# Moving h and the second layer's head outputs within SBUF in a float32 two-layer backbone

## The chip, the cores and the metric

The kernel runs on one core of a Trainium2 chip. The metric is the device time of one execution in microseconds (us), the median of several runs. The engines are named as the profile names them: PE is TensorE's products and PEld its weight loads, DVE is VectorE, ACT is ScalarE, POOL is GpSimd, SP is SyncE, whose queue issues most of the DMA transfers. SBUF is the on-chip memory of 128 partitions that products read their operands from, PSUM the memory that they write to.

## The reference, cut to what matters

Two layers over 512 latent tokens `x` and 256 context tokens `ctx`, 1024 channels each. The first layer mixes by gated linear attention, the second by an mLSTM; each ends in a convolutional feed-forward block (ConvFFN). All of it is float32.

```
for i in range(2):
    h_c = rmsnorm(ctx, ...) * (1 + sc1_c) + sh1_c          # modulated norms
    h_l = rmsnorm(x, ...)   * (1 + sc1_l) + sh1_l
    o_c, o_l = gla_mixer(h_c, h_l, ...) if i == 0 else mlstm_mixer(h_c, h_l, ...)
    x = x + g1_l * o_l                                     # a mixer ends in (heads * gate) @ w_out
    h_l = rmsnorm(x, ...) * (1 + sc2_l) + sh2_l
    x = x + g2_l * conv_ffn(h_l, ...)                      # (gelu(conv(h @ w_g)) * (h @ w_a)) @ w_down
    ...                                                    # layer 0: the same for ctx
return rmsnorm(x, final_norm_g)
```

The mixers' inputs (queries, keys, values, gates of 4 heads) are products of h with columns of one large matrix. `w_g` and `w_a` are 1024 x 2816, `w_down` is 2816 x 1024.

## The kernel before

**Products.** Activations lie channel-major: the partition is the channel within a block of 128, the free axis is the token, 256 context tokens first and then 512 latent ones. A float32 product is made of three passes over operands split in two (hi and lo): `mm3` (lines 308 to 310) issues hi by hi, hi by lo, lo by hi. In `nc.tensor.matmul(ps, l, r)` the first operand is the stationary one, 128 columns that a weight load (PEld) brings into PE, and the second the moving one, of 256 or 512 columns here. While PE streams one product it loads the next one's weights.

**h** is the modulated norm, held as two tiles `hhi_` and `hlo_` of [128, 8, 768] float32 (`new_h`). For `projT_steps` the moving operand is row k of h over the latent tokens (512 columns, 1,024 bytes into the row) or over the context (256 columns, at the row's begin), and the weights are stationary. For the values (`v_proj`, and `values` at the start) it is the other way: 128 tokens of h are stationary, the weights move.

**Where tiles lie.** Pools are handed out from the bottom of SBUF, each tile at a multiple of 32 bytes. The constants' pool (`self.pc`) starts at byte 16,512 of a partition with `ident` (512 bytes), `ones` (128), `eps` and `junk` (32 each); then come `xl` (16,384), `xc` (8,192), `hhi_` and `hlo_` (24,576 each), and behind them the small tables, `A01` and `mgb` among the last. Then comes the pool of the large weights, with slots of 4,096 bytes. A row of h has 3,072 bytes and a block of 128 weight columns 512, so within 512 bytes all rows of a tile, both token ranges and all weight blocks begin at the same place. The places that matter, by the program's own allocation:

| tile | used by | first byte | place within 512 |
|---|---|---|---|
| `hhi_`, `hlo_` (h) | `fg`, `fa`, `fs`, `fsc`, `gr`, `gk`, `gq`, `mk`, `mq`, `mo` move it; the values keep it stationary | 41,792 and 66,368 | 320 |
| rings `whi`, `wlo` (large weights) | stationary for the products just named but half of `fs`, `fsc`; stationary for the output projections of heads 0 to 2 | 107,936 on | 416 |
| `ahi`, `alo` and `wh_d`, `wl_d` (layer 0) | moving and stationary of `fd`; half of `fs`, `fsc` has its weights in `wh_d`'s ring | 189,632 and 150,720 on | 192, both |
| the same, layer 1 | the same | 188,576 and 149,664 on | 160, both |
| `hhi`, `hlo` of the heads, layer 0 | moving in the output projection `po` | 215,968 on | 416 |
| `hhi`, `hlo` of the heads, layer 1 | the same | 212,224 on | 256 |
| `xl`, `xc` (the residual) | no product's operand | 17,216 and 33,600 | 320 |

Head 3's output projection has its weights in slots of other tiles (96 in the first layer; 320, 0 and 96 in the second).

**Names of products.** In the ConvFFN `fg` is h by the gate weights and `fa` h by the value weights, for each of 22 blocks of 128 channels; `fs` and `fsc` are the same for the first two blocks (latent halves and context); `fd` is the down product. In the first layer's scans `gk`, `gq`, `gr` are keys, queries and the output gate of a head, in the second's `mk`, `mq`, `mo`; `vpsgv` and `vpsmv` are the values, `v01p` those of heads 0 and 1 at the start. `po` is the output projection; its number gives layer, head and block, its letter the tokens (`L` all 512 latent ones, `C` the context).

**Order.** PE's order is the program's. In the mixers the steps of a head's scan are interleaved by hand with other products (`Filler`): values, output gate, queries and keys of the next head, and the last head's output projection. In the ConvFFN, `up` issues the gate products of a block, the convolution on VectorE (9 steps of 512 columns, line 1418), the value products, and every few blocks `down`, whose results VectorE adds to the residual (`update`, line 553). Three PSUM banks serve the down products, so a late update holds PE up.

Of the kernel before, what the change touches and what calls it, by code (L numbers as in the profile page):

```python
"""Two-layer hybrid backbone (gated linear attention, then mLSTM, each with a ConvFFN).

Activations are kept channel-major: partition = channel within a block of 128, free = token.
Float32 products run as three float32r passes: x = hi + lo is an exact split, and
hi*hi + hi*lo + lo*hi carries float32's accuracy.
"""
# [18 lines left out]
P = 128  # L25
D = 1024
KT = D // P
# [16 lines left out]
# the table set with both Exp and Ln  # L44
EXP_LN = "natural_log_exp_and_others"
# share of products between two steps of a scan, by head
# [9 lines left out]
class TwoPools:  # L56
    """One pool to its users; tiles whose tag is listed come from the first pool."""
# [8 lines left out]
class Filler:  # L66
    """Products (generators that yield a rough weight) to run between the steps of a scan.

    A step of side, which waits for its own loads, comes in after each share of `every`."""
# [21 lines left out]
    def through(self, gen):  # L91
        """Run up to the end of gen."""
        while gen in self.gens:
            self.step()
        self.owed = min(self.owed, 0.0)
# [13 lines left out]
class Norm:  # L109
    """rms norm of one 256-token segment in steps that the products of other segments run between."""  # L110
# [7 lines left out]
    def square(self, k):  # L118
        """Squares summed over blocks 0..6, and those of block 7."""
        nc = self.b.nc  # L120
        acc = self.acc[k == KT - 1]
        if k in (0, KT - 1):
            nc.scalar.activation(acc, self.xs[k], AF.Square)
            return
        sq = self.tail.sq[k % 2]
        nc.scalar.activation(sq, self.xs[k], AF.Square)
        (nc.vector if k > 4 else nc.gpsimd).tensor_tensor(acc, acc, sq, op=ALU.add)

    def stat(self, spread=True):
        """1/rms of the tokens: columns of r and, on every partition, PSUM rb [128, 256]."""  # L130
# [15 lines left out]
    def mod(self, k):  # L146
        """Block k of h: normalised x, modulated and split."""
# [22 lines left out]
    def gain(self, k):  # L170
        """Block k times the final gain, turned token-major."""
# [8 lines left out]
    def store(self):  # L180
        """Output rows of the segment: the turned blocks over the rms of their token."""
# [12 lines left out]
class Tail:  # L194
    """The last residual update of a phase, by segments, and the norms that follow it."""
# [14 lines left out]
    def after(self, si, m):  # L210
        """Called when block m of segment si has been updated."""
# [16 lines left out]
        else:  # L228
            # what the segment before left, then its successor's
# [6 lines left out]
class Body:  # L236
# [14 lines left out]
    def start_tile(self, name):  # L251
        """Any of the six banks that the start has for its tiles."""
        self.turn = (self.turn + 1) % 6
        return self.mm_tile(name) if self.turn < 4 else self.aux_tile(name)
# [12 lines left out]
    def split(self, hi, lo, src, bias=None, eng=None):  # L267
        """hi + lo = src (+ bias), exactly; hi, lo are float32r."""
# [8 lines left out]
    def load_w(self, src, name, kind="", bufs=3, later=False, more=None, eng=None):  # L277
        """Weight block src [nk*128, C], and columns more of the same rows, as split [128, nk, C] tiles;
        eng takes the differences."""
# [12 lines left out]
    def w_tile(self, pool, dt, tag, name, bufs, nk, C):  # L292
        """[128, nk, C] in a slot of 1024 columns."""
# [11 lines left out]
    def mm3(self, ps, wl, wr, start, stop):  # L305
        """ps += lhs^T rhs for split operands (hi, lo)."""
# [5 lines left out]
    def projT_steps(self, ps, w, h, cols):  # L312
        """ps [128, n] = (h @ w)^T over the KT blocks; w [128, KT, 128], h [128, KT, TOK]."""
# [9 lines left out]
    def vec_table(self, rows, name, pool=None):  # L323
        """rows: list of DRAM APs [n, 128]; returns a [128, sum n] tile of columns."""
        return self.vec_turn(*self.vec_load(rows, name, pool=pool))
# [62 lines left out]
    def run_late(self, n=9):  # L388
        """Steps of the last norm that were left to the phase that follows."""
# [5 lines left out]
    def ada_setup(self):  # L395
# [7 lines left out]
        self.A = {}  # L403

    def ada_load(self, l, blks, k0, nk, pool):
        """Rows k0.. (nk blocks) of the modulation columns blks."""
# [25 lines left out]
    def ada_piece(self, l, blks, pool, sts):  # L432
        """Modulation blocks blks (4 blocks of 128 channels) of layer l for both streams.

        Column group j of the tensor engine takes block j, so four products run at once."""
# [10 lines left out]
        # block j of the list sits in columns 32 j + stream  # L446
# [7 lines left out]
    def ada_seq(self, parts):  # L454
        """Modulation parts (layer, part) in halves of 512 columns, one row block of weights per step, loaded
        two steps ahead: the rows times their entries of c are summed over the row blocks for each stream, then
        over the partitions on the tensor engine.

        Parts: 0 sh1, 1 sc1, 2 g1, 3 sh2, 4 sc2, 5 g2."""
# [11 lines left out]
        for i, (l, part, half, k) in enumerate(steps):  # L471
# [3 lines left out]
            # the context needs no more after the second layer's mixing  # L475
# [12 lines left out]
            # column group j: blocks 2 q and 2 q + 1 of stream s for j = 2 q + s, or block j of the one stream  # L488
# [27 lines left out]
    def make_A(self, l, which, b0, n, ns=2):  # L516
        """A = g * (1 + sc) for n channel blocks from b0, the first ns streams."""
# [17 lines left out]
    def inv_sqrt(self, r, ss, n):  # L535
        """r = (ss / n + eps) ** -0.5"""
# [4 lines left out]
    def sqrt_next(self, t):  # L541
        """Have the root's table loaded once t, the last result of another function, is there."""
        self.nc.scalar.activation(self.junk, t[:, -1:], AF.Sqrt, bias=self.eps, scale=0.0)

    def x_seg(self, seg):
        """Residual blocks of a 256-token segment: 0, 1 the latent halves, 2 the context."""
# [4 lines left out]
    def update(self, xv, ps, gate):  # L551
        """x += gate * ps"""
        self.nc.vector.scalar_tensor_tensor(xv, ps, gate, xv, op0=ALU.mult, op1=ALU.add)  # L553

    def start(self, pool):
        """The first layer's h, two channel blocks at a time as their modulation comes in; the values of
        heads 0 and 1 are summed up over the blocks on the way. The second half of the latent tokens comes
        in last. Returns the PSUM tiles of the values and the last steps of their sums, one for each pair
        of chunks."""
        nc = self.nc  # L560
        # x over the rms, channel-major: columns ctx, then latent
# [16 lines left out]
        def squares(seg):  # L578
            ss[seg] = pool.tile([P, 2], F32, tag="xss", name=f"xss{seg}", bufs=3)
            for t in range(2):  # L580
                # the squares themselves go where xr comes, in blocks that are still free
# [18 lines left out]
        def spread(*segs):  # L600
            """1/rms on every partition."""
# [12 lines left out]
        def modulate(i, *parts):  # L614
            """Blocks 2 i and 2 i + 1 of h for parts (stream, columns) that lie side by side."""
# [63 lines left out]
    def out_weights(self, l, h, to=None):  # L679
        """Per block of 128 rows: (hi, lo), each two [128, 512] views; to: eight views to take them."""  # L680
# [16 lines left out]
    def out_proj(self, l, h, acts, segs, tail=None, w=None):  # L697
        """x += g1 * (act @ w_out) over the rows of head h; acts[h]: (hi, lo) lists of two blocks."""
# [25 lines left out]
    def head_square(self, pool, l, h, o, p):  # L724
        """Sum of squares of pair p of token-major o."""
        if p == 0:
            self.ss = pool.tile([P, NPAIR], F32, tag="hss", name=f"hss{l}{h}", bufs=2)
        sq = pool.tile([P, DV], BF16, tag="hsq", name=f"hsq{l}{h}{p}", bufs=1)
        self.nc.scalar.activation(sq, o[:, p, :], AF.Square, accum_out=self.ss[:, p:p + 1])

    def head_norm(self, pool, l, h, o, npair):
        """Token-major o [128, npair, DV] of a head over its rms, in place."""
# [6 lines left out]
    def head_gate(self, pool, l, h, o, npair, gate, g, bufs, acts, segs=None):  # L739
        """o transposed, times g and the gate; split into acts[h]. segs: (pair, pairs) to finish one by one."""  # L740
# [29 lines left out]
    def v_proj(self, vt, w_in, col0, name, gates=None):  # L770
        """Token-major values of one head: vt [128, NPAIR, >=DV]. With gates (first column, number, out): those
        columns' products as well, handed to out(p, ps) for each pair of chunks p."""
# [21 lines left out]
    def gla_masks(self, pc):  # L794
        """Keep token j for output i: forward j <= i, backward j >= i; scores are [j, i]."""
# [9 lines left out]
    def scan_mask(self, pool):  # L805
        """1 everywhere, 0 where a chunk starts: for the forward and the backward scan."""
# [6 lines left out]
    def gla_za(self, keep, pool):  # L813
        """Low-rank gate inputs, split and stacked for one product: rows hi, lo, hi."""
        nc, a = self.nc, self.a
        # in the rings of the large weights
# [21 lines left out]
        # gate weights: rows hi, hi, lo; the other direction's rows are zero  # L838
# [10 lines left out]
    def gla_gates(self, pool, h, zs, w2, smask):  # L849
        """exp(+-c), c the log decay of each direction summed from the middle of each pair of chunks,  # L850
        and the factors that carry the state from one pair to the next."""
# [19 lines left out]
        # sums of whole chunks; the half that comes first in its direction counts from its end  # L871
# [4 lines left out]
        # order of pairs 1, 0, 5, 4, 3, 2; g[p] leads out of pair p  # L876
# [18 lines left out]
    def gla_qk(self, pool, h, gates, hats):  # L895
        """Queries and keys of a head, scaled by the decay of each direction, over the gates."""
# [31 lines left out]
    def gla_scan(self, pool, h, hats, vt, steps, scb, free):  # L928
        """Both directions of one head; yields where other products may run. free() makes o's slot free."""
# [67 lines left out]
    def gla(self, vps, last):  # L997
        with ExitStack() as es:
# [10 lines left out]
            with self.tc.tile_pool(name="gla_b", bufs=1) as hpb:  # L1009
# [14 lines left out]
                for h in range(NH):  # L1024
# [14 lines left out]
                    if h == NH - 1:  # L1039
                        # into slots that the last heads have left, to keep the ring of weights for the next phase  # L1040
# [516 lines left out]
```

## Time and profile before

| | |
|---|---|
| median of 3 runs | 1664.98 us (1663.76 to 1666.72) |
| profiled execution: span from the first to the last instruction | 1662.1 us |
| mean granted TensorE clock | 0.992 |
| PE busy | 1625.9 us (98%) |
| VectorE busy | 1256.2 us (76%) |
| ScalarE busy | 673.3 us (41%) |
| first layer's ConvFFN, main part | 440 to 950 us |
| second layer's ConvFFN, main part | 1296 to 1631 us |

The profile gives one execution. Its span leaves out what lies before the first and behind the last instruction; the runs' median is 2.9 us above it. Products are pipelined and the profile models their ends, so the time that a product costs in a stream is the distance from its start to the next one's start, not its listed duration.

### The profile page before, as it was taken

Reading aid. Unit: us, or ns where it says so; the run is one execution under the profiler, and the core shown is the slowest. Engines: PE = TensorE matmul, PEld = TensorE weight load, DVE = VectorE, ACT = ScalarE, POOL = GpSimd, SP = SyncE. Lnnn points to the kernel's source line nnn. Section 1 sums busy time; section 2 is a strip of 40 time slices with the busy share of each in tenths; the row PEclk is TensorE's granted clock in tenths of the full one; section 3 lists DMA queues with packets and bytes.
Section 4 is the critical chain, followed back from the end, with each engine's and each line's share of the span. In section 5 each row is a group of like instructions: output and inputs, shape, how many; then the busy total and the mean of one; then the engine's idle time right before and its main releaser. Section 6 shows DMA issues by size and latency. Waiting matters only on the chain.

```text
span 1662.1 us, 24173 instructions
## 1 busy us (share of the span) xinstructions
PE 1625.9 (98%) x9504; PEld 1398.3 (84%) x9504; DVE 1256.2 (76%) x2139; ACT 673.3 (41%) x1155; POOL 109.2 (7%) x174
## 2 busy tenths in 40 slices
PE   7999999998999999999999999999998999999998
PEld 6778898888988888888888998889878877888887
DVE  5867877868975978686666589776778898777874
ACT  5675444446431314132221366635465333222334
POOL 0011001004000000000000130000002110000001
PEclk9999999999999999999999999999999999999999
DMA  9522443522330523251222125243321233223321
GB/s 311 173 59 72 146 135 109 159 70 60 93 108 26 152 77 115 65 170 53 75 64 65 39 78 151 83 134 102 90 63 51 77 114 102 75 77 102 114 77 51
DMA packets 178614, 163.64 MB, mean 98 GB/s; under 512 B 8860, under 2 KB 146724, under 8 KB 178500
## 3 DMA queue, kind: packets, MB, share of 16 engines
q1 hardware_dynamic: 178132, 161.97, 32.1%
q8 instruction: 74, 1.21, 0.3%
q14 instruction: 40, 0.33, 0.1%
q10 hardware_dynamic: 240, 0.13, 0.0%
q0 software_dynamic: 128, 0.00, 0.0%
HBM read 159.98 MB, written 2.10 MB: 98 GB/s over the span
## 4 chain that ended last, share of the span: by engine, by line
PE 84%; DVE 9%; ACT 4%; issue 1%; DMA 1%; POOL 1%; DVEq 0%; ACTq 0%; POOLq 0%
PE fd L308 6%; PE fd L309 6%; PE fd L310 6%; PE fa L308 5%; PE fa L309 5%; PE fa L310 5%; PE fg L308 5%; PE fg L310 5%; PE fg L309 5%; DVE acc L1418 2%; PE vpsmv L308 1%; PE vpsmv L310 1%; PE vpsmv L309 1%; PE op L990 1%; PE mu L1278 1%
## 5 line engine op out<-in xcount | busy, mean ns | idle before, releaser
L1418 DVE SCALAR_TENSOR_TENSOR acc<-gp,vt_f,acc 128x512 f32<-128x512 f32 x352 | 263.3, 758 | 4.3
L308 PE MATMUL fd<-ahi,wh_d 128*128 128x512 f32 (+1 forms) x584 | 198.4, 340 | 4.9 <-DVE xl L553 4.8
L310 PE MATMUL fd<-ahi,wl_d 128*128 128x512 f32 (+1 forms) x584 | 197.7, 339 | 0.0
L309 PE MATMUL fd<-alo,wh_d 128*128 128x512 f32 (+1 forms) x584 | 197.5, 338 | 0.0
L484 DVE SCALAR_TENSOR_TENSOR asum<-ast,sil,asum 128x512 f32<-128x512 f32 x224 | 163.6, 756 | 21.8 <-ACT asum L481 13.7
L308 PE MATMUL fa<-hhi,wh_a 128*128 128x512 f32 (+1 forms) x480 | 172.2, 359 | 0.0
L308 PE MATMUL fg<-hhi,wh_g 128*128 128x512 f32 (+1 forms) x480 | 172.1, 359 | 0.0
L310 PE MATMUL fa<-hhi,wl_a 128*128 128x512 f32 (+1 forms) x480 | 171.7, 358 | 0.0
L309 PE MATMUL fa<-hlo,wh_a 128*128 128x512 f32 (+1 forms) x480 | 171.6, 358 | 0.0
L310 PE MATMUL fg<-hhi,wl_g 128*128 128x512 f32 (+1 forms) x480 | 171.6, 358 | 0.0
L309 PE MATMUL fg<-hlo,wh_g 128*128 128x512 f32 (+1 forms) x480 | 171.6, 357 | 0.0
L553 DVE SCALAR_TENSOR_TENSOR xl<-fd,mod,xl 128x512 f32<-128x512 f32 (+1 forms) x136 | 92.8, 685 | 74.1 <-PE fd L310 74.0
L308 PEld LDWEIGHTS fd<-ahi,wh_d 128*128 128x128 f32 x584 | 111.1, 190 | 18.2 <-DVE xl L553 6.2
L310 PEld LDWEIGHTS fd<-ahi,wl_d 128*128 128x128 f32 x584 | 111.0, 190 | 12.0 <-DVE wl_d L272 0.2
L309 PEld LDWEIGHTS fd<-alo,wh_d 128*128 128x128 f32 x584 | 111.0, 190 | 11.7
L1419 ACT ACTIVATE acc<-acc,vt_f 128x256 f32<-128x256 f32 (+1 forms) x66 | 42.8, 652 | 167.9 <-DVE acc L1418 167.1
L308 PEld LDWEIGHTS fa<-hhi,wh_a 128*128 128x128 f32 x480 | 90.4, 188 | 15.6 <-issue 0.6
L308 PEld LDWEIGHTS fg<-hhi,wh_g 128*128 128x128 f32 x480 | 90.4, 188 | 15.5 <-issue 1.0
L310 PEld LDWEIGHTS fg<-hhi,wl_g 128*128 128x128 f32 x480 | 90.3, 188 | 14.7
L310 PEld LDWEIGHTS fa<-hhi,wl_a 128*128 128x128 f32 x480 | 90.4, 188 | 14.6
L309 PEld LDWEIGHTS fa<-hlo,wh_a 128*128 128x128 f32 x480 | 90.4, 188 | 14.6
L309 PEld LDWEIGHTS fg<-hlo,wh_g 128*128 128x128 f32 x480 | 90.4, 188 | 14.5
(1438 smaller groups left out, 3827.3 us busy)
## 6 DMA issues: line engine op xcount, KB each, us to landing
ast<-in_ada_w_dram SPq DMA_DIRECT2D x160, 256.0 KB
st_g<-in_ffn_w_up_dram SPq DMA_DIRECT2D x44, 512.0 KB
st_a<-in_ffn_w_up_dram SPq DMA_DIRECT2D x44, 512.0 KB
st_d<-in_ffn_w_down_dram SPq DMA_DIRECT2D x44, 512.0 KB
ast<-in_ada_w_dram SPq DMA_DIRECT2D x16, 512.0 KB
st_wo<-in_gla_w_out_dram SPq DMA_DIRECT2D x14, 512.0 KB
st_gr<-in_gla_w_in_dram SPq DMA_DIRECT2D x8, 512.0 KB
st_mo<-in_mlstm_w_in_dram SPq DMA_DIRECT2D x8, 512.0 KB
```

Of the source, the lines that this page charges most:

```text
L308: nc.tensor.matmul(ps, wl[0], wr[0], start=start, stop=False)
L309: nc.tensor.matmul(ps, wl[0], wr[1], start=False, stop=False)
L310: nc.tensor.matmul(ps, wl[1], wr[0], start=False, stop=stop)
L484: nc.vector.scalar_tensor_tensor(acc[s], st, c[s], acc[s], op0=ALU.mult, op1=ALU.add)
L553: self.nc.vector.scalar_tensor_tensor(xv, ps, gate, xv, op0=ALU.mult, op1=ALU.add)
L990: nc.tensor.matmul(op[:, :DV], l_, r_, start=(i == 0), stop=False)
L1278: nc.tensor.matmul(u[:, :DV + 1], kt[d, s], vt[:, p, :], start=True, stop=True)
L1418: nc.vector.scalar_tensor_tensor(o, s, tw, o, op0=ALU.mult, op1=ALU.add)
L1419: nc.scalar.activation(acc[:, c0:c0 + n], acc[:, c0:c0 + n], AF.Gelu_apprx_tanh, bias=cb[:, c:c + 1])
```

## The change

Two constants' tiles are allocated at the begin of the constants' pool, ahead of x and h: `A01` (64 bytes) and `mgb` (4 bytes, 32 with the gap). Both came behind h before, so what lies between moves up by 96 bytes, h and x among it, and everything behind stays where it was. In the second layer the scratch tile of `head_square` gets 80 more bfloat16 columns that nothing uses (160 bytes), which moves the head outputs behind it by 160 bytes. By the sizes h comes to 416 within 512 bytes, `xl` and `xc` to 416, the second layer's head outputs to 416. No instruction is added or removed. The new file also blanks comments and docstrings, which is left out here.

```
     def consts(self):
...
         self.junk = pc.tile([P, 1], F32, tag="junk", name="junk")
+        self.A = {(0, 1): pc.tile([P, KT, 2], F32, tag="A01", name="A01")}
+        self.mgb = pc.tile([P, 1], F32, tag="mgb", name="mgb")
...
     def ada_setup(self):
...
         self.mod = [pc.tile([P, 48, 2], F32, tag=f"mod{l}", name=f"mod{l}") for l in range(2)]
-        self.A = {}
...
     def head_square(self, pool, l, h, o, p):
...
-        sq = pool.tile([P, DV], BF16, tag="hsq", name=f"hsq{l}{h}{p}", bufs=1)
+        sq = pool.tile([P, DV + 80 * l], BF16, tag="hsq", name=f"hsq{l}{h}{p}", bufs=1)[:, :DV]
...
     def ml_gate_bias(self):
         nc = self.nc
-        self.mgb = self.pc.tile([P, 1], F32, tag="mgb", name="mgb")
         nc.gpsimd.memset(self.mgb, 0.0)
```

## Rows read from the trace of the kernel before

**Rows 1.** The page: busy time by engine; the chain that ended last.
```profile
PE 1625.9 (98%) x9504; PEld 1398.3 (84%) x9504; DVE 1256.2 (76%) x2139; ACT 673.3 (41%) x1155; POOL 109.2 (7%) x174
...
PE 84%; DVE 9%; ACT 4%; issue 1%; DMA 1%; POOL 1%; DVEq 0%; ACTq 0%; POOLq 0%
```

**Rows 2.** Windows: stretch, its length, busy time by engine, granted clock, DMA.
```profile
0.00:75.00 75.00, 64.53 (x513) 48.55 (x514) 49.18 (x100) 42.76 (x76) 5.97 (x19) 1.00 0.78 251
...
440.00:950.00 510.00, 510.00 (x2992) 445.61 (x2991) 364.48 (x574) 138.15 (x218) 4.45 (x6) 1.00 0.28 84
...
1010.00:1247.00 237.00, 235.50 (x1353) 199.70 (x1352) 181.14 (x397) 128.67 (x228) 7.11 (x24) 1.00 0.33 100
...
1296.00:1372.00 76.00, 73.20 (x307) 58.39 (x306) 73.24 (x91) 27.35 (x36) 12.07 (x4) 0.98 0.35 104
1372.00:1631.00 259.00, 257.20 (x1111) 208.76 (x1111) 197.54 (x263) 74.55 (x94) 0.00 (x0) 1.00 0.29 88
```

**Rows 3.** Waits of PE, 1296 to 1372 us: total, times, longest.
```profile
PE fd L308 <- DVE xl L553: 2.8, 1, 2.8
```

**Rows 4.** Chain that ended last, in order of time: start, length, what.
```profile
235.28 3.23 DMA ast<-in_ada_w_dram
...
249.16 1.65 DVE ge L868
...
1306.54 7.54 DVE acc L1418 x9
```

**Rows 5.** Timeline of PE, 438 to 448 us: start, length, product.
```profile
438.82 0.39 PE L308 MATMUL fg<-hhi,wh_g 128*128 128x512 f32 x1
...
444.44 0.28 PE L308 MATMUL fg<-hhi,wh_g 128*128 128x256 f32 x1
...
447.29 0.40 PE L308 MATMUL fa<-hhi,wh_a 128*128 128x512 f32 x1
```

**Rows 6.** Timeline of PE, 506 to 523 us, the first `fd` of each width.
```profile
506.42 0.39 PE L308 MATMUL fd<-ahi,wh_d 128*128 128x512 f32 x1
...
522.78 0.28 PE L308 MATMUL fd<-ahi,wh_d 128*128 128x256 f32 x1
```

**Rows 7.** Timeline of PE, 282 to 286 us, output projection of the first layer.
```profile
282.50 0.39 PE L309 MATMUL po012L<-hlo,wh_wo 128*128 128x512 f32 x1
...
286.13 0.39 PE L310 MATMUL po014L<-hhi,wl_wo 128*128 128x512 f32 x1
```

**Rows 8.** Timeline of PE, 1245 to 1250 us, output projection of the second layer.
```profile
1245.64 0.40 PE L309 MATMUL po125L<-hlo,wh_wo 128*128 128x512 f32 x1
...
1249.61 0.38 PE L751 MATMUL hps<-ident,mlo 128*128 128x128 f32 x2
```

**Rows 9.** Groups of PE by shape: line, product, count, busy us and mean ns, idle.
```profile
L308 PE MATMUL fa<-hhi,wh_a 128*128 128x512 f32 x320 | 127.0, 397 | 0.0
...
L308 PE MATMUL fa<-hhi,wh_a 128*128 128x256 f32 x160 | 45.1, 282 | 0.0
...
L308 PE MATMUL mo<-hhi,wh_mo 128*128 128x512 f32 x64 | 28.3, 442 | 0.0
L308 PE MATMUL gr<-hhi,wh_gr 128*128 128x512 f32 x64 | 27.8, 434 | 0.0
```

**Rows 10.** Timeline of PE, two runs of 48 products of 256 columns.
```profile
227.28 0.28 PE L308 MATMUL po000C<-hhi,wh_wo 128*128 128x256 f32 x1
...
233.02 0.26 PE L340 MATMUL vp_f<-ident,vr_f 110*128 110x110 f32 x1
...
427.43 0.28 PE L308 MATMUL fsc<-hhi,wh_g 128*128 128x256 f32 x1
...
433.07 0.28 PE L308 MATMUL fsc<-hhi,wh_g 128*128 128x256 f32 x1
```

**Rows 11.** Groups of DVE by shape, 440 to 950 us and 1400 to 1600 us.
```profile
L1418 DVE SCALAR_TENSOR_TENSOR acc<-gp,vt_f,acc 128x512 f32<-128x512 f32 x165 | 123.1, 747 | 1.9
...
L1418 DVE SCALAR_TENSOR_TENSOR acc<-gp,vt_f,acc 128x512 f32<-128x512 f32 x96 | 71.8, 748 | 1.7
```

More of the change, by code (lines that the diff above doesn't have):

```diff
@@ L264, in consts @@
         self.junk = pc.tile([P, 1], F32, tag="junk", name="junk")
+        self.A = {(0, 1): pc.tile([P, KT, 2], F32, tag="A01", name="A01")}
+        self.mgb = pc.tile([P, 1], F32, tag="mgb", name="mgb")
     def split(self, hi, lo, src, bias=None, eng=None):
@@ L402, in ada_setup @@
         self.mod = [pc.tile([P, 48, 2], F32, tag=f"mod{l}", name=f"mod{l}") for l in range(2)]
-        self.A = {}
     def ada_load(self, l, blks, k0, nk, pool):
@@ L727, in head_square @@
             self.ss = pool.tile([P, NPAIR], F32, tag="hss", name=f"hss{l}{h}", bufs=2)
-        sq = pool.tile([P, DV], BF16, tag="hsq", name=f"hsq{l}{h}{p}", bufs=1)
+        sq = pool.tile([P, DV + 80 * l], BF16, tag="hsq", name=f"hsq{l}{h}{p}", bufs=1)[:, :DV]
         self.nc.scalar.activation(sq, o[:, p, :], AF.Square, accum_out=self.ss[:, p:p + 1])
@@ L1057, in ml_gate_bias @@
         nc = self.nc
-        self.mgb = self.pc.tile([P, 1], F32, tag="mgb", name="mgb")
         nc.gpsimd.memset(self.mgb, 0.0)
```

## The prediction, made before the change was run

> **What bounds the kernel now.** First the page's first and fourth parts [rows 1]: in them the reader is to see that TensorE (PE) is busy for 98% of the 1662.1 us span, and that 84% of the chain that ended last is PE. So a change of the pace at which PE takes its products can reach the end, but only where PE sets the pace. Second, the busy times by stretch [rows 2]: in the first layer's ConvFFN (440 to 950 us) PE is never idle while VectorE has 145.5 of 510 us free; the second layer's scans (1010 to 1247) and the rest of its ConvFFN (1372 to 1631) look alike, with 1.5 and 1.8 us of PE idle. Two stretches differ. Up to 75 us PE is idle for 10.5 us. From 1296 to 1372 VectorE is busy for 73.2 of 76 us, and there the waits show PE standing 2.8 us for a residual update that queues behind VectorE's convolutions [rows 3]. Third, the chain in order of time [rows 4]: in the first layer's scans a transfer and the gates' VectorE work lie on it at 235 and 249 us, in the early second ConvFFN the convolutions. Full pace elsewhere is not the clock's doing: the granted share is 1.00 in nearly all of these stretches, the higher of the two levels, 2.4 GHz.
>
> Fourth, the pace itself. Starts of back-to-back products are closer together than one product lasts, so I read start to start, and set beside each the two places of its operands within 512 bytes from the table of the section on the kernel.
> - `fg`, moving operand at 320, weights at 416: 24 products from 438.82 to 444.44 us, 5.62 us, 234.2 ns each [rows 5].
> - `fd`, both at 192: 72 products from 506.42 to 522.78, 16.36 us, 227.2 ns each [rows 6].
> - The output projection is one piece of code with two layouts. First layer, both at 416: 16 products from 282.50 to 286.13, 226.9 ns [rows 7]. Second layer, 256 against 416: 17 products from 1245.64 to 1249.61, 233.5 ns [rows 8].
>
> So equal places go with 227 ns, unequal ones with 234 ns, and the last pair says that it isn't a matter of `fd` against `fg`.
>
> **The change part by part.** No instruction is added, removed or reordered; two small tiles of constants, `A01` and `mgb`, are allocated ahead of x and h, not behind them, and one scratch tile of the second layer's heads is 160 bytes longer. That puts h (and x, by the way) at 416 where it was at 320, and the second layer's head outputs at 416 where they were at 256. The large weights stay at 416.
>
> *512-column products.* Those that become equal, per line of the three-pass product and then times 3 [rows 9]: `fa` and `fg` 320 each, 1920 together; `gr` 64, `gk` and `gq` half as many each, 384; `mo` 64, `mk` and `mq` half as many each, 384; the second layer's output projection of three heads, 3 heads x 8 blocks x 2 x 3 passes, 144; the start's values, 6 chunks x 8 blocks x 3, 144, where h is the stationary operand. Sum 2976. Price: 234.2 - 227.2 = 7.0 ns by `fg` against `fd`, 6.6 by the output projection; I take 7.0, as the larger sample. 2976 x 7.0 ns = 20.8 us.
>
> *256-column products.* Here the rows point the other way. Equal places: the output projection over the context, both at 416, 48 products from 227.28 to 233.02 us, 119.6 ns [rows 10]. Unequal: `fsc`, h at 320 against 416, 48 products from 427.43 to 433.07, 117.5 ns [rows 10]; but `fg` over the context, with the same two places, takes 24 from 444.44 to 447.29, 118.8 ns [rows 5]. So the loss lies between 0.8 and 2.1 ns, and as two unequal readings differ by 1.3 ns, I don't exclude none. I take 2.0, nearer to the longer sample. The count: `fa` and `fg` 160 each per line, 960; `gr`, `gk`, `gq` over the context 384; `mk` 96; of the first blocks of both ConvFFNs the half whose weights lie at 416, 144 and 96. Sum 1680, times 2.0 ns = 3.4 us lost. The values' products, whose moving operand is the weight, and everything on the tiles at 96, 160 or 192 I leave at nothing: no equal pair comes or goes there but the values' (720 products); a nanosecond on them is 0.7 us.
>
> *The other tiles that move.* x goes from 320 to 416, so VectorE's and ScalarE's accesses start elsewhere. The rows let me cost this at nothing: the same convolution step takes 747 ns with its sum at 192 (first layer) and 748 ns at 160 (second) [rows 11]. Were it more, VectorE's free time in the long stretches covers it; without that cover 1 ns on each of some 500 such operations is half a microsecond.
>
> *Where the saving stays.* Net of both prices, by stage:
> - Start: 144 x 7.0 = 1.0 us. PE waits for others there: counted at nothing.
> - First layer's scans: 384 x (7.0 - 2.0) = 1.9 us. The chain runs over a transfer and the gates as late as 249 us, past the middle of these scans [rows 4]; PE would come earlier to what VectorE hands it. Counted half: 1.0.
> - First ConvFFN: 960 x 5.0 - 144 x 2.0 = 4.5 us, counted whole: PE has no idle time there.
> - Second layer's scans: 528 x 7.0 - 96 x 2.0 = 3.5 us. The first head's 48 of `mk` and `mq` run ahead of the scans, beside the gate rows' VectorE work, and I drop their 0.3: 3.2.
> - Second ConvFFN: 960 x 7.0 - 96 x 2.0 = 6.5 us. The first 5 blocks, 240 products and 1.7 us, run while VectorE sets the pace; what PE gains becomes a longer wait for the residual update. 4.8 to 4.9 remain.
>
> Counted: 1.0 + 4.5 + 3.2 + 4.85 = 13.5 us of 17.4. The profiled span of 1662.1 would be 1648.6; the runs' median stands 2.9 us above that span, so 1664.98 - 13.5 = 1651.4 us. The sum's own ends: every gain kept and no loss on 256 columns, 1644.1; 6.6 ns, 2.1 ns lost and the two long ConvFFN stretches alone (960 and 720 of the 512s, 960 of the 256s), 9.1 us, 1655.9.
>
> A rule of the Trainium skill speaks against the whole: its page "SBUF — State Buffer", section "SBUF: two separate sides", holds that TensorE's port never waits on anyone, and the page "TensorE: Matmul & The Clock Gate" (Part 2) gives the moving operand and the weight load a read port each. By that a start address moves nothing and the sum is zero. The pair of output projections, one code at 226.9 and 233.5 ns, disagrees.
>
> **The rivals.**
> - *The place is not the cause* (time 1665.0, no change). For it: no row shows h itself at an equal place. Against it: all four readings at 512 columns sort by it, the two output projections among them. [...] Chance 0.07.
> - *Slower: equal places cost at both widths.* The 512-column difference would come from something else that `fd` and the first layer's projection share, and the 2.0 ns of the 256-column rows would hold for h at 512 too: (2976 + 1680) x 2.0 = 9.3 us, 1674.3. It decides as soon as the 512-column products gain less than 3.4 us / 2976 = 1.1 ns each. For it: the 256-column rows. Against it: a 6.6 ns gap in one code. Chance 0.05.
> - *The scans swallow their share* (1655 to 1656): only the two long ConvFFN stretches keep their gain, as in the lower end above, because products between scan steps only fill time until VectorE or ScalarE is ready. For it: the chain at 235 and 249 us. Against it: 1.5 us of PE idle in 237 in the second layer's scans. Chance 0.15.
> - *All is kept* (1644 to 1648): the 256-column loss doesn't come, or the early stages gain with PE. Chance 0.08.
> - The forecast, 1651.4, within 1648 to 1655: chance 0.65.
>
> **How the numbers follow.** A measurement of this kernel tells a difference of about 0.2%, 3.3 us. Faster by more: the forecast, the swallowed scans and the full gain, 0.88. Within: mostly the first rival, 0.07. Slower: 0.05. The range leaves out the two rivals above 1664 and the outermost of the sum's ends: 1645 to 1657.
>
> **What would show it.** In the profile of the changed kernel `fg`, `fa`, `gr`, `mo` and the second layer's `po` must run at 227 ns from start to start, `fd` unchanged; the context's `fg` and `fsc` near 120 ns; the stretch of the first ConvFFN about 4.5 us shorter; the wait for the residual update at about 1331 us longer by about 1.7 us. If h's products stay at 234 ns, the reading of the places is wrong. If they run at 227 and the span is shorter by less than 9 us, the gain went into waits that I took for slack. The granted clock is the other danger: in 1296 to 1372 its mean is 0.98, not 1.00; a longer wait of PE there may bring one more spell at 1.2 GHz, which costs little while VectorE sets the pace but shows in the end if it falls later.

## The result, and the profile after

The changed kernel takes 1652.17 us (median of 4 runs, 1651.38 to 1654.31); the kernel before, with one more run, 1665.64 us (median of 4, 1663.76 to 1666.72). The ratio is 0.9923, 95% interval 0.9911 to 0.9935: faster, by 13.5 us by the medians.

From the page after, the lines that answer to [rows 1]:

```profile
PE 1609.5 (98%) x9504; PEld 1397.0 (85%) x9504; DVE 1253.4 (76%) x2139; ACT 672.8 (41%) x1155; POOL 109.9 (7%) x174
...
PE 83%; DVE 9%; ACT 4%; DMA 2%; issue 1%; POOL 1%; DVEq 0%; ACTq 0%; POOLq 0%
```

The counts are the same, and the other engines are busy for as long as before within 3 us. PE alone lost 16.4 us of busy time. The span is 1650.6 us, 11.5 less than before's 1662.1.

**The pace.** PE's timeline in the first ConvFFN, answering to [rows 5], and at the end of the second layer's output projection, answering to [rows 8]: start, length, product.

```profile
438.15 0.40 PE L312 MATMUL fg<-hhi,wh_g 128*128 128x512 f32 x1
...
443.60 0.28 PE L312 MATMUL fg<-hhi,wh_g 128*128 128x256 f32 x1
...
446.47 0.40 PE L312 MATMUL fa<-hhi,wh_a 128*128 128x512 f32 x1
...
1240.99 0.40 PE L313 MATMUL po125L<-hlo,wh_wo 128*128 128x512 f32 x1
...
1244.86 0.82 PE L755 MATMUL hps<-ident,mlo 128*128 128x128 f32 x6
```

Read start to start: 24 products of 512 columns in 5.45 us, 227.1 ns each, where they took 234.2; 24 of 256 columns in 2.87 us, 119.6 ns, where they took 118.8; the 17 of the output projection in 3.87 us, 227.6 ns, where they took 233.5. `fd` stays as it was, 72 products from 504.85 to 521.18, 226.8 ns against 227.2 [rows 6].

**Where the time went.** To compare stages I cut both spans at the starts of the same products, so that a row of the one and a row of the other hold the same work. Busy time by stretch of the kernel before, cut that way (stretch, length, PE, PEld, DVE, ACT, POOL, granted clock, DMA share, GB/s):

```profile
0.00:75.21 75.21, 64.75 (x513) 48.71 (x514) 49.39 (x100) 42.97 (x76) 5.97 (x19) 1.00 0.78 250
75.21:371.05 295.84, 292.81 (x1793) 253.97 (x1792) 230.05 (x394) 145.65 (x266) 26.68 (x40) 1.00 0.36 109
371.05:440.23 69.18, 64.81 (x509) 62.80 (x507) 61.99 (x131) 37.24 (x82) 19.46 (x24) 0.95 0.29 83
440.23:950.10 509.87, 509.87 (x2992) 445.52 (x2990) 364.25 (x573) 138.02 (x217) 4.45 (x6) 1.00 0.28 84
950.10:1010.10 60.00, 58.83 (x418) 55.12 (x417) 49.78 (x103) 39.55 (x73) 15.34 (x33) 0.97 0.31 93
1010.10:1247.05 236.95, 235.45 (x1352) 199.61 (x1351) 181.07 (x398) 128.72 (x228) 7.11 (x24) 1.00 0.33 100
1247.05:1296.18 49.13, 44.87 (x334) 42.79 (x332) 34.16 (x65) 22.88 (x51) 12.30 (x16) 0.93 0.15 44
1296.18:1373.86 77.68, 73.08 (x306) 58.25 (x305) 74.97 (x94) 27.17 (x35) 12.07 (x4) 0.98 0.35 102
1373.86:1631.20 257.34, 257.34 (x1111) 208.92 (x1111) 195.88 (x260) 74.75 (x94) 0.00 (x0) 1.00 0.29 88
```

The same stages of the changed kernel, answering to [rows 2]:

```profile
0.00:75.24 75.24, 64.66 (x513) 48.87 (x514) 49.54 (x100) 42.88 (x76) 5.97 (x19) 1.00 0.78 250
75.24:370.96 295.72, 292.21 (x1793) 254.54 (x1791) 230.17 (x394) 145.48 (x266) 27.09 (x40) 1.00 0.36 109
370.96:439.52 68.56, 62.41 (x509) 60.41 (x507) 61.79 (x131) 36.94 (x82) 19.56 (x24) 1.00 0.29 84
439.52:945.22 505.70, 505.70 (x2992) 447.10 (x2990) 363.22 (x573) 138.40 (x218) 4.42 (x6) 1.00 0.29 84
945.22:1005.06 59.84, 57.63 (x417) 53.73 (x416) 49.48 (x103) 39.58 (x73) 15.29 (x33) 1.00 0.31 93
1005.06:1242.36 237.30, 235.50 (x1353) 201.15 (x1351) 181.32 (x398) 128.46 (x228) 7.12 (x24) 0.99 0.33 99
1242.36:1290.65 48.29, 43.99 (x333) 42.04 (x332) 34.01 (x65) 22.93 (x51) 12.78 (x16) 0.96 0.15 45
1290.65:1367.90 77.25, 71.60 (x306) 58.06 (x304) 73.79 (x94) 27.15 (x35) 11.79 (x4) 0.98 0.35 103
1367.90:1619.66 251.76, 251.76 (x1110) 208.48 (x1111) 195.38 (x260) 74.69 (x94) 0.00 (x0) 1.00 0.31 90
```

Line by line, the lengths differ by 0.0, -0.1, -0.6, -4.2, -0.2, +0.4, -0.8, -0.4 and -5.6 us; what is left to the end is equal. The two long ConvFFN stretches carry 9.8 of the 11.5 us. The start gains nothing. The first layer's scans gain nearly nothing, and the second layer's look as if they had become longer.

That last row is partly the clock. One product of the values, in the kernel before and in the changed one:

```profile
1020.01 0.29 PE L308 MATMUL vpsmv<-wh_mv,hhi 128*128 128x256 f32 x1
```

```profile
1016.69 0.28 PE L312 MATMUL vpsmv<-wh_mv,hhi 128*128 128x256 f32 x1
```

At the stage's begin the changed kernel is 5.04 us ahead (1010.10 against 1005.06), here only 3.32. Between lies a spell at the lower of the two clock levels, 1.2 GHz, that the other execution doesn't have; in the changed kernel's windows PE is busy for half of the 3.3 us before it and all through it:

```profile
1005.00:1008.30 3.30, 1.58 (x15) 1.33 (x15) 3.17 (x9) 0.37 (x1) 0.00 (x0) 0.99 0.32 83
1008.30:1011.60 3.30, 3.30 (x17) 3.30 (x17) 3.30 (x9) 0.00 (x0) 0.13 (x2) 0.50 0.40 100
```

It costs 1.7 us (5.04 - 3.32); the rest of the stage gains 1.4. The kernel before has the same half-idle stretch there, and no drop came in that execution:

```profile
1010.00:1013.00 3.00, 1.50 (x15) 1.26 (x14) 2.87 (x9) 0.37 (x1) 0.00 (x0) 1.00 0.32 84
1013.00:1017.00 4.00, 4.00 (x35) 4.00 (x35) 4.00 (x11) 1.00 (x2) 0.13 (x2) 1.00 0.46 135
```

In the third, fifth and seventh rows it goes the other way: the granted clock is 0.95, 0.97 and 0.93 before against 1.00, 1.00 and 0.96, and these stages are 1.6 us shorter together. Such spells fall differently in each execution. If all of the 1.6 us is put down to them, which no run shows by itself, they cancel here against the 1.7, and the change is worth 11.6 us between these two executions.

### The profile page after: what moved, and what is told of

Its sections match the earlier page's. It is cut to its first block, busy times and chain, and to the rows that moved or that the text cites. A ratio compares the mean times of both kernels' runs of the same rounds, so it can differ in the third digit from the quotient of the medians.

```text
span 1650.6 us, 24173 instructions
## 1 busy us (share of the span) xinstructions
PE 1609.5 (98%) x9504; PEld 1397.0 (85%) x9504; DVE 1253.4 (76%) x2139; ACT 672.8 (41%) x1155; POOL 109.9 (7%) x174
## 4 chain that ended last, share of the span: by engine, by line
PE 83%; DVE 9%; ACT 4%; DMA 2%; issue 1%; POOL 1%; DVEq 0%; ACTq 0%; POOLq 0%
PE fd L312 6%; PE fd L313 6%; PE fd L314 6%; PE fa L312 5%; PE fg L312 5%; PE fg L313 5%; PE fa L313 5%; PE fa L314 5%; PE fg L314 5%; DVE acc L1421 2%; PE op L994 1%; PE gr L314 1%; PE gr L313 1%; PE gr L312 1%; PE vpsmv L314 1%
## 5 line engine op out<-in xcount | busy, mean ns | idle before, releaser
L314 PEld LDWEIGHTS fg<-hhi,wl_g 128*128 128x128 f32 x480 | 90.7, 189 | 12.6
```

What stands on the lines that cost most here:

```text
L314: nc.tensor.matmul(ps, wl[1], wr[0], start=False, stop=stop)
```

## The experiments

The theory: a float32 product of 512 columns is faster by 7 ns when its moving operand and its weights begin at the same place. Rivals: it is h's new place by itself, or x's, or the constants'; and for the size of the place's period, a span other than 512 bytes.

**Each move by itself.** The first kernel has the two constants' tiles moved and the heads' scratch as before; the second has only the scratch tile:

```
# e1_h_only: only these
+        self.A = {(0, 1): pc.tile([P, KT, 2], F32, tag="A01", name="A01")}
+        self.mgb = pc.tile([P, 1], F32, tag="mgb", name="mgb")
# e2_heads_only: only this
-        sq = pool.tile([P, DV], BF16, ...)
+        sq = pool.tile([P, DV + 80 * l], BF16, ...)[:, :DV]
```

> Only h (and x) moves to 416; the second layer's head outputs stay at 256. If equal places of the two operands set the pace: fg and fa at 227 ns as in the changed kernel, the second layer's output projection back at 234 ns, time 1652.2 + 144 x 4 to 7 ns = 1652.8 to 1653.2 us. If the gain came from the head outputs or from something that h's move doesn't bring: 234 ns for fg, 1665 us.

> Only the second layer's head outputs move to 416; h stays at 320. Equal places: fg and fa at 234 ns, the second layer's output projection at 227 to 229 ns, 144 x 4 to 7 ns = 0.6 to 1.0 us gained at most, time 1664.6 to 1665.1 us, no difference that can be measured. If the head outputs carried more of the gain: 1660 us or less.

h alone: 1653.87 us, 0.7 over the expected, ratio 0.9943 (0.9929 to 0.9957); `fg` at 227.1 ns (24 from 440.52 to 445.97), the second layer's output projection still at 233.5 (17 from 1241.98 to 1245.95). The heads alone: 1664.37 us, 0.9999 (0.9990 to 1.0008); `fg` at 234.2, the projection at 227.5. Each product follows its own tile. The heads' 144 products are worth 0.9 us by the pace, less than the runs can tell.

**The weights moved away, h left in its new place.** A pad behind the modulation table shifts the ring of large weights, and all tiles behind, but not h. With 96 bytes h stays at 416 and the weights come to 0; the heads, which shift too, stay equal to their weights.

```
# on the changed kernel, in ada_setup, behind self.mod (24 floats: 96 bytes)
+        pc.tile([P, 24], F32, tag="pad", name="pad")
```

> The change in full, but 96 unused bytes behind h move the large weights, and all behind them, from 416 to 0: h at 416 is again 96 bytes away from them, the head outputs of both layers stay equal to their weights (all at 0). If equal places set the pace: fg and fa back at 234 ns, the context's fg at 117 to 119 ns, the output projections at 227 to 229 ns, time 1664 to 1666 us. If h's own place at 416 is what counts: fg at 227 ns, 1652 us.

Measured 1663.79 us, 0.9998 (0.9989 to 1.0007): the whole gain is gone. PE's timeline of this kernel:

```profile
440.14 0.39 PE L312 MATMUL fg<-hhi,wh_g 128*128 128x512 f32 x1
...
445.76 0.28 PE L312 MATMUL fg<-hhi,wh_g 128*128 128x256 f32 x1
```

24 products in 5.62 us, 234.2 ns, with h, x and the constants exactly where the changed kernel has them. So their own place is not the cause. The output projection, equal here, ran at 227.5 ns.

**The weights moved to h instead.** The kernel before with a pad of 416 bytes at the same spot: h stays at 320, the weights come to 320, the second layer's heads to 160.

```
# on the kernel before, same spot
+        pc.tile([P, 104], F32, tag="pad", name="pad")
```

> The kernel before with 416 unused bytes behind h: h stays at 320 and the large weights come to 320 as well; the second layer's head outputs (at 160) stay unequal to them. If equal places set the pace, wherever they are: fg and fa at 227 ns, the context's fg near 120 ns, the second layer's output projection at 234 ns, time 1652.5 to 1653.5 us. If h's own place counts: 234 ns, 1665 us.

Measured 1652.79 us, 0.9930 (0.9916 to 0.9944), as fast as the changed kernel. PE's timeline of this kernel:

```profile
439.40 0.40 PE L308 MATMUL fg<-hhi,wh_g 128*128 128x512 f32 x1
...
444.85 0.28 PE L308 MATMUL fg<-hhi,wh_g 128*128 128x256 f32 x1
...
1241.18 0.41 PE L309 MATMUL po125L<-hlo,wh_wo 128*128 128x512 f32 x1
...
1245.16 0.38 PE L752 MATMUL hps<-ident,mlo 128*128 128x128 f32 x2
```

227.1 ns for `fg`, and in one trace with it 234.1 for the unequal projection (17 in 3.98 us). It is the distance between the two operands, not an absolute place.

**How equal, and within what.** The same pad on the changed kernel in five other sizes: 32, 64, 128, 192 and 256 bytes (8, 16, 32, 48 and 64 floats). If the period is 512 bytes, 256 must be slow; if it is 64 or 128, those must be fast.

> The change in full and 32 unused bytes behind h: the weights at 448, h at 416, 32 apart. Equality within 512 bytes: 234 ns for fg, 1663 to 1666 us. Every distance tried so far is an odd multiple of 32, so equality within 64 bytes says 234 ns here too.

> 64 unused bytes behind h: weights at 480, h at 416, 64 apart. Equality within 512 bytes: fg at 234 ns, 1663 to 1666 us. Equality within 64 bytes (the finest span that the readings so far allow): 227 ns, 1652 us.

> 128 unused bytes behind h: weights at 32, h at 416, 128 apart. Equality within 512 or 256 bytes: fg at 234 ns, 1663 to 1666 us. Equality within 128 or 64 bytes: 227 ns, 1652 us.

> 256 unused bytes behind h: weights at 160, h at 416, 256 apart. Equality within 512 bytes: fg at 234 ns, 1663 to 1666 us. Equality within 256 bytes or less: 227 ns, 1652 us.

> 192 unused bytes behind h: the weights at 96, h at 416, so h lies 64 bytes above the weights counted within 256 bytes, where the run with 64 bytes had it 64 below. Equality within 256 bytes: fg at 232 to 234 ns. If the context's products gain from a distance of 64 bytes whichever way it goes: 114 to 115 ns and about 1657 us; if the side counts: 117 to 120 ns and 1662 to 1665 us.

Measured, with `fg` from the first run of 24 products of each width behind the norms (starts are read to 0.01 us, so a pace is good to 0.4 ns), and "h behind weights" the distance from the weights' place up to h's, within 256 bytes:

| kernel | h behind weights | median us | ratio (95%) | 512 columns, ns | 256 columns, ns |
|---|---|---|---|---|---|
| changed | 0 | 1652.17 | 0.9923 (0.9911 to 0.9935) | 227.1 | 119.6 |
| pad 256 | 0 | 1651.00 | 0.9920 (0.9891 to 0.9949) | 227.1 | 120.0 |
| pad 192 | 64 | 1653.32 | 0.9932 (0.9911 to 0.9953) | 229.2 | 117.9 |
| pad 128 | 128 | 1664.35 | 0.9993 (0.9980 to 1.0005) | 232.9 | 118.3 |
| pad 96 | 160 | 1663.79 | 0.9998 (0.9989 to 1.0007) | 234.2 | 118.8 |
| pad 64 | 192 | 1657.11 | 0.9959 (0.9939 to 0.9979) | 233.3 | 113.3 |
| pad 32 | 224 | 1662.68 | 0.9984 (0.9973 to 0.9996) | 233.3 | 117.9 |

PE's timeline with 256 bytes, then with 64:

```profile
439.51 0.40 PE L312 MATMUL fg<-hhi,wh_g 128*128 128x512 f32 x1
...
444.96 0.28 PE L312 MATMUL fg<-hhi,wh_g 128*128 128x256 f32 x1
```

```profile
438.36 0.39 PE L312 MATMUL fg<-hhi,wh_g 128*128 128x512 f32 x1
...
443.96 0.28 PE L312 MATMUL fg<-hhi,wh_g 128*128 128x256 f32 x1
...
446.68 0.39 PE L312 MATMUL fa<-hhi,wh_a 128*128 128x512 f32 x1
```

With 256 bytes between them the operands are unequal within 512, and the product is fast all the same. With 64 or 128 it is slow. So it is equality within 256 bytes that counts, not within 512. Nor is it only equal or unequal: 64 bytes one way is nearly as good (229.2; I had expected 232 to 234, a miss, and the time of 1653.32 us lies below both expected ones), 64 the other way is not. And at 256 columns the order is another one: the 64 bytes that are slow at 512 columns are the fastest there, 2.72 us for 24. So the kernel with the 64-byte pad has a time that neither expectation gave: by the medians of its own comparison it is 8.0 us faster than the kernel before (1657.11 against 1665.15) with `fg` at 233.3.

The values show which way the distance is to be counted, as in them the weights move and h is stationary. 48 of them in the kernel with 192 bytes, then in the one with 64:

```profile
1011.01 0.28 PE L312 MATMUL vpsmv<-wh_mv,hhi 128*128 128x256 f32 x1
...
1016.45 0.28 PE L312 MATMUL vpsmv<-wh_mv,hhi 128*128 128x256 f32 x1
```

```profile
1010.12 0.28 PE L312 MATMUL vpsmv<-wh_mv,hhi 128*128 128x256 f32 x1
...
1015.77 0.28 PE L312 MATMUL vpsmv<-wh_mv,hhi 128*128 128x256 f32 x1
```

That is 113.3 ns with 192 bytes and 117.7 with 64, where `fg` has 117.9 and 113.3. At 512 columns the start's values ran at 233.5 and 230.0 ns, where `fg` has 229.2 and 233.3. Each pace belongs to one distance of the moving operand behind the stationary one, whichever of the two is h.

**The scans with their fill products behind them.** Why did the scans keep so little? A row of `gr` in the changed kernel, between two steps of the scan:

```profile
171.16 0.40 PE L313 MATMUL gr<-hlo,wh_gr 128*128 128x512 f32 x1
...
172.09 0.39 PE L314 MATMUL gr<-hhi,wl_gr 128*128 128x512 f32 x1
...
174.13 0.40 PE L314 MATMUL gr<-hhi,wl_gr 128*128 128x512 f32 x1
```

The first product behind the break takes 0.31 us to the next one's start. The four distances behind it are 232.5 ns each (0.93 us), the next nine 226.7 (2.04 us). A stream cut into short rows would then gain less. To test it, both kernels were run with the shares of products between scan steps at zero, so that each scan's fill products follow it in one piece:

```
-FILL0 = (1.6, 3.2, 3.2, 1.7)
-FILL1 = (1.6, 1.6, 1.6, 0.8)
+FILL0 = (0.0, 0.0, 0.0, 0.0)
+FILL1 = (0.0, 0.0, 0.0, 0.0)
```

> The kernel before with the shares of products between two scan steps at zero: each head's scan runs bare and its other products follow in one piece. The partner of the next run. gr, mo, gk and gq at 234 ns in all their length; the time grows by some tens of us, as bare scans wait for their own chain.

> The changed kernel with the same zero shares. In the changed kernel gr and mo gained 3 ns apiece, not 7. If the cause is that they are interrupted by scan products and the first ones behind a break keep the slower pace, they are now at 227 to 228 ns in their long runs, and the scans' two stretches are together 4 to 5 us shorter than in the run without the change (912 products at 6 to 7 ns, less 480 at 2 ns). If the scans' products as such gain less, 230 ns stays. If what PE gains is waited away, the pace is 227 ns and the stretches are as long as without the change.

Measured: the kernel before so filled 1670.86 us, 1.0040 (1.0026 to 1.0053); the changed one 1656.14, 0.9949 (0.9933 to 0.9965); 14.7 us between them. The first grew by 6.3 us, not by some tens. The edit did less than it was meant to: of the 768 products of 512 columns of the six kinds, those behind the fifth of their row rose from 341 to 437 only, because many products stay between a scan's own steps, and `gr` lies in 46 rows where it lay in 34, only three of them of 24. Such a row of `gr` in the changed kernel so filled:

```profile
189.72 0.40 PE L312 MATMUL gr<-hhi,wh_gr 128*128 128x512 f32 x1
...
195.19 0.28 PE L312 MATMUL gr<-hhi,wh_gr 128*128 128x256 f32 x1
```

It takes 5.47 us, 227.9 ns each, against 234.2 for the same 24 in its partner, so in a long row `gr` gains 6.3 ns. The two layers' scans, cut at the same products, in the first of these kernels and in the second (each has one spell at half the clock in its second row):

```profile
75.08:371.08 296.00, 292.21 (x1759) 249.79 (x1761) 229.58 (x396) 142.96 (x265) 25.68 (x40) 1.00 0.36 107
1010.15:1247.14 236.99, 234.23 (x1333) 196.90 (x1332) 176.08 (x393) 127.54 (x224) 6.89 (x28) 0.99 0.34 100
```

```profile
73.14:368.30 295.16, 291.15 (x1760) 250.29 (x1761) 229.45 (x396) 142.99 (x265) 25.74 (x40) 1.00 0.36 107
1002.62:1237.91 235.29, 232.21 (x1333) 196.84 (x1332) 176.23 (x394) 127.47 (x224) 6.92 (x28) 0.99 0.33 100
```

0.8 and 1.7 us, 2.5 together, where the interleaved kernels have 0.1 and 1.4. Over all distances between neighbours of one kind, without waits, `gr` gains 4.8 ns here (234.0 to 229.2) and 3.4 interleaved (233.8 to 230.4), `mo` 4.9 and 3.4. The breaks are part of it; the 4 to 5 us that this theory had put on the scans didn't come, with most of the short rows still there.

**The context tokens at another distance.** As 512 and 256 columns want different distances, one more kernel takes latent and context tokens of h, and of the first ConvFFN's activations, into tiles of their own: the latent h equal to the weights, the context's 64 bytes before them.

```
# on the changed kernel; Halves hands out the tile that the columns lie in
+        ctx = [pc.tile([P, KT, CTX], F32R, tag=f"h{x}c_", ...) for x in ("hi", "lo")]
+        if (0, 1) not in self.A:
+            self.A[(0, 1)] = pc.tile([P, KT, 2], F32, tag="A01", name="A01")
+        lat = [pc.tile([P, KT, SEQ], F32R, tag=f"h{x}_", ...) for x in ("hi", "lo")]
+        self.h = tuple(Halves(c, l) for c, l in zip(ctx, lat))
...
+                    if not c0 and c == 0:
+                        pool.tile([P, 112], F32, tag="apad", name="apad")      # 448 bytes
...
+                    hi = pool.tile([P, n], F32R, tag=f"ahi{x}", ...)       # x: "c" for the context
+                    lo = pool.tile([P, n], F32R, tag=f"alo{x}", ...)
```

> The changed kernel with latent and context tokens in tiles of their own, for h and for the first ConvFFN's activations: the latent ones at the place of their weights (227 ns for 512 columns), the context ones 64 bytes below it, where the run with 64 bytes showed 114 to 117 ns for 256 columns. The start's split takes 8 more short VectorE operations. If the two readings add up: the context's fg and fa 960 x 5 ns = 4.8 us, fd over the context 528 x 5 ns = 2.6 us, some 700 others 1 to 2 us, less what the scans don't pass on: 1644 to 1646 us. If 64 bytes apart only helps where all of h lies there: fg over the context near 120 ns and 1651 to 1653 us.

Measured 1649.79 us (1649.04 to 1653.37), 0.9909 (0.9895 to 0.9923), between the two expected times: the lowest median of the study, 2.4 us under the changed one's, with overlapping intervals. The first ConvFFN, cut at the same products, of the changed kernel and of this one:

```profile
440.20:950.01 509.81, 509.81 (x3029) 451.33 (x3028) 365.44 (x579) 140.47 (x222) 5.88 (x8) 1.00 0.28 84
```

```profile
443.19:949.19 506.00, 506.00 (x3029) 447.91 (x3028) 364.86 (x580) 140.59 (x222) 5.89 (x8) 1.00 0.29 84
```

3.8 us less. The context's `fg` went from 119.7 to 117.3 ns over all neighbours of one kind, `fd` from 119.9 to 118.1. The 114.6 of the 64-byte pad, over the same neighbours, didn't come, though the distance is the same. Rows of the context's h lie 1,024 bytes apart here and 3,072 there, but that alone is not the reason: `gk` over the same context rows came to 115.1 (119.5 in the changed kernel, 114.2 with the 64-byte pad). What keeps `fg` back is open. In the profiled execution, the slowest of the five, the start took back 4.2 us, with a spell at half the clock from 75.2 to 78.6 us in it and the split of h in eight more VectorE operations.

## Why the prediction was right, and where its sum was not

- *The place is the cause.* Right, and shown: moving h alone, the heads alone, the weights away and the weights to h, the 512-column products went with the distance each time, within one trace too. Only the period was wrong: 256 bytes. All pairs that the prediction compared are equal or unequal in both, so that nothing hung on it. By the rule of the Trainium skill that it cited ("SBUF — State Buffer", "SBUF: two separate sides"), that TensorE's port never waits on anyone, the prediction worked out that a start address moves nothing; these runs don't agree with that, with 227 against 234 ns for the same product. Whether a port waits in it, no row shows.
- *7.0 ns for 512 columns.* Right in unbroken streams. Over all neighbours of one kind `fg` and `fa` went from 234.1 to 227.6 and 227.9 in the first layer, from 234.2 to 226.7 in the second.
- *2.0 ns lost at 256 columns.* Right: `fg` and `fa` over the context from 117.7 and 117.8 to 119.7 over all neighbours, and the 48 of `fsc` from 117.5 to 119.8.
- *The values and x at nothing.* The values went from 119.8 to 119.6 ns, VectorE's update of x has a mean of 748 ns before and after, and the convolution step one of 753 (758 before). No stage shows a loss beyond the clock's spell.
- *The start at nothing.* Right (0.0), though its own products ran at 229.7 instead of 233.8 ns: others set that stage's end.
- *First ConvFFN 4.5.* Measured 4.2.
- *Second ConvFFN 4.85.* Measured 0.4 + 5.6 = 6.0. The step held in kind: where VectorE sets the pace PE's gain became waits. PE's waits from 1290 to 1372 us, answering to [rows 3]:

```profile
PE fd L312 <- DVE xl L556: 5.4, 2, 3.1
```

  Before, from 1290 to 1380 us, the same two waits:

```profile
PE fd L308 <- DVE xl L553: 4.6, 2, 2.8
```

  So the wait grew by 0.8, not 1.7, and the stage kept 0.4 that the prediction had given up. The stretch behind it gained 7.7 ns per product, not 7.0 (5.58 us over 720).
- *The scans 1.0 and 3.2.* This is the term that was mis-sized. Measured 0.1 and, without the clock's spell, 1.4: 1.5 us instead of 4.2. The step took 384 and 528 products at the full 7.0 ns. They don't have it: `gr` and `mo` gained 3.4 and 3.4 ns, `gk` and `gq` 4.9 and 4.4, and only `mk` and `mq`, in longer rows, 6.2 and 6.6. The rows behind a break and the long row of the runs with zero shares show one cause of it. By these paces and 1.2 to 2.1 ns lost on their 256-column products, the scans should still have kept about 1.0 and 2.1 us; of the other 0.9 and 0.7, PE's idle time took 0.5 and 0.3 (in the rows of the stages it grew from 3.0 to 3.5 and from 1.5 to 1.8 us), and the rest is open: with the zero shares they kept 2.5 us. In the first layer the chain had the gates' VectorE work and a transfer, which the prediction counted at half; no run took these away.
- *The total.* By stages the counted 13.5 us became 11.6. The forecast met the median because of what it was set against. It took the median as 2.9 us above the profiled span; but the changed kernel's profiled execution took 1652.32 us for a span of 1650.6, 1.7 above. By that, before's span of 1662.1 belongs to an execution of about 1663.8, the lowest of its runs (1663.76), while the median was 1665. So 13.5 us between medians and 11.5 between the profiles are the same change seen through a scatter of 1 to 2 us, and the agreement to 0.8 us is luck in part: the sum itself was 2 us too high. Against the 21 runs of the kernel before that were made beside the next experiments, with a median of 1664.73 us, the change is worth 12.6 us.
- *The rivals.* "Place not the cause" and "equal places cost at both widths" fell with the first trace. "The scans swallow their share" came true in its effect, for nearly two thirds of the 4.2 us, but less by its mechanism: by the paces 2.0 of the 5.1 us that the prediction's prices gave the scans never arose, and 0.8 us became idle time. Its time (1655 to 1656) didn't come, as both ConvFFNs together kept 10.2 us, not 9.1, and the medians are 13.5 us apart where the profiled spans are 11.5.

## What to carry to other kernels

Where back-to-back products bound a kernel, read start to start and set the pace beside the operands' addresses: here a shift of 96 bytes, with no instruction changed, was worth 0.8%, and any later change of a tile's size ahead of them can take it back unseen. Gains per product read in a long stream hold for long streams; count the products in broken rows at what such rows show. Make a sum against the profiled execution's own time, and give the runs' scatter (here the medians of the kernel before lie between 1664.55 and 1665.64 us, single executions up to 7 us apart) before you take an agreement as proof.

## What the runs showed of the hardware

- The pace of a 512-column float32 product depends on the distance of its moving operand behind its stationary one within 256 bytes: 227 ns at 0, 229 at 64, 233 to 234 at 96 (the unequal output projections), 128, 160, 192 and 224.
- At 256 columns the order differs: 119.6 at 0, 117.9 at 64, 113.3 at 192, 118 to 119 at 128, 160 and 224. At 192 it didn't come for `fg` in the last kernel (117.3). What sets it is open.
- Behind a break the first four or so 512-column products run at 232 ns even at equal places, where later ones run at 227 (the row of `gr` from 170.84 us).
- Executions of one kernel spread by up to 7 us (1661.0 to 1668.2 with the 96-byte pad). In the profiled ones, between two and seven spells at 1.2 GHz lie before the last norms. They come mostly at a few places (at about 20, 400, 974, 1010, 1250 and 1330 us, and once each at 70, 75 and 1369), in one execution at these and in another at those; the one compared above cost 1.7 us.
